# Norm of k and the turns of b, k and v: from the matrix engine to VectorE and 32-partition transfers, in a two-layer hybrid trunk

## The chip, the cores and the metric

The kernel runs on one core of one Trainium2 chip. Time is device microseconds of that core, the median of several runs; the profile is one execution recorded by the hardware profiler. The engines are TensorE (PE, with its weight loads PEld), VectorE (DVE), ScalarE (ACT), GpSimd (POOL) and SyncE (SP, which here only issues transfers).

## The reference, cut to what matters

The input x has 512 rows of 1024 features. Each of two layers runs a norm, one wide projection into all branches, three branches side by side (RWKV-7 time mixing, chunked retention, a spatial gating unit), a gated merge with an output projection, and a gated MLP with a depthwise convolution. The change lies in the RWKV-7 branch (8 heads of 64):

```python
kk = (k * k_k).astype(jnp.float32)
k = k * (1.0 + (a - 1.0) * k_a)
...
kk = kk / jnp.maximum(jnp.sqrt(jnp.sum(kk * kk, axis=-1, keepdims=True)), 1e-12)
y = rwkv7_scan(r, decay, k, v, kk, a)
...
sa = jnp.einsum('bhvk,bhk->bhv', state, -kk_t)
state = (state * w_t[:, :, None, :]
         + sa[..., None] * (kk_t * a_t)[:, :, None, :]
         + v_t[..., None] * k_t[:, :, None, :])
y = jnp.einsum('bhvk,bhk->bhv', state, r_t)
```

So kk is normed by head and time step, and the state is updated 512 times, one step after the other.

## The kernel before, in words

Activations lie with features on the 128 partitions and the 512 time steps along the free axis. Every large product is made three times in a rounded format (`mm3`, L147 to L157: the products of L151, for the parts hi and lo of both sides). A weight unit of 128 x 512 is loaded by SP (`load`, L121, three raw buffers), cut into hi and lo by ACT (L134) and DVE (L135) ahead of its use (`part`), and read by twelve products.

`run` goes through both layers; `mixer` calls `rwkv`. There, a pair of heads (m = 0 to 3) has its columns r, k, v from `cols3(m)`, and `prep(m)` makes the decays, the scaled operands `x` (L494, L495), `bk` (b and k, L498 and L501) and, with TensorE (L507, L510), the products of b and k with the operands by chunks of 64 steps. In `prep`, ACT squares k (L476) into `kkn`; four TensorE products with a matrix of two columns of ones per half sum the squares by head (L479), with the time steps on the partitions; DVE bounds the sums from below into `nw` (L480). After the fourth prep DVE writes the reciprocals into `n2` (L553), by 32-step blocks.

`solve` (L671) inverts the 64 x 64 triangles of all chunks and heads. DVE transposes the blocks (L696) and the norms (L698), scales with them (L699), runs 31 elimination steps (L703, L705), scales again (L706) and transposes back (L708, L710); ACT and POOL copy the diagonal blocks out and in (`diag`, L684, L686). Then TensorE makes two sets of 64 small products (L720, L729), with copies between them.

Then comes the recurrence, chunk by chunk (c = 0 to 7; L581 to L650). It needs b, k and v with time on the partitions. `vpair(c)` turns v of two chunks by four TensorE transposes (L568) into a PSUM bank, from which ACT copies with the halves swapped (L573); per chunk four transposes turn b and k (L590), and ACT copies them out (L601, L603). Small products of `mm` (L563) then do, in each chunk: the products of the state St with `x`; a copy of the result into `xb` by DVE (L599); the products of `xb`, of k and of v; a copy into `U` by ACT (L617); the products of `U`; the state update by DVE (L626, or L628 and L629). The output y is copied by ACT (L633) and normed every two chunks by DVE, with a power on POOL (L648).

Between these small steps `fill` puts units of other work, mostly the gate projections (`gates`), into PE's queue: 35 half-steps during the solve, which may move, and fixed ones of twelve products between the steps of a chunk. The gates go to memory by ACT's queue (L380) and come back in `merge` by POOL's (L934). A planner lays out the instructions of all engines from its own estimated costs; `tc.keep_in_program_order` (`po`) pins an instruction behind the one written just before it on the same engine. The engines then run each queue in that order. Tiles of one tag share a fixed number of buffers: `cs` three, `r` sixteen.

In layer 1's up-projection `turn_x` (L958 to L969) already turns blocks of x: DVE transposes of 32 x 32 blocks (L963), SP transfers to memory (L966) and back in 128-byte pieces (L968).

Of the kernel before, what the change touches and what calls it, by code (L numbers as in the profile page):

```python
# [47 lines left out]
class Emit:  # L48
# [346 lines left out]
    def rwkv(self, l, nst):  # L395
# [15 lines left out]
        n2, nw = self.small((128, 32), "n2"), self.small((128, 4, 4, 2), "nw")  # L411
        Ws = []
        for i in range(2):
            wua, s = self.u(n="wua"), self.u(dt=F32R, n="wus")
# [45 lines left out]
        def prep(m):  # L460


            k, r, v = kc[m], rc[m], Vf[m]
            ms = slice(m * 128, m * 128 + 128)
            pL, pA = self.sm(), self.sm()
            for o, w, (xh, xl) in zip((pL, pA), Ws, Xs):
                T.matmul(o, w[:, ms], xl, start=True, stop=False)  # L467
                T.matmul(o, w[:, ms], xh, start=False, stop=True)  # L468
# [7 lines left out]
            A.activation(kkn, k, AF.Square, scale=self.p("kk", m))  # L476
            pn = self.sm((128, 4, 2))
            for i in range(4):
                T.matmul(pn[:, i, :], kkn[:, i * 128:i * 128 + 128], self.c("bones2"), start=True, stop=True)  # L479
            V.tensor_scalar(nw[:, m], pn, 1e-24, None, op0=MAX)  # L480
            A.activation(ld, pL, AF.Tanh, scale=0.5, bias=haw[:, 4 + m:5 + m])
            A.activation(ld, ld, AF.Identity, scale=-0.5 * EXP_HALF, bias=self.c("ehalf"))
            V.tensor_tensor_scan(ci, self.rst, ld, 0.0, op0=MUL, op1=ADD)
# [12 lines left out]
            V.scalar_tensor_tensor(kkn, tha, 1.0, k, op0=ADD, op1=MUL)  # L496
            A.activation(tha, tha, AF.Identity, scale=hka[:, m:m + 1], bias=oka[:, m:m + 1])
            V.scalar_tensor_tensor(bk[:, :, 0, :], q8(kkn), nkk[:, m:m + 1], q8(Eout), op0=MUL, op1=MUL)  # L498
            kp = k
            V.tensor_tensor(kp, k, tha, op=MUL)  # L500
            V.tensor_tensor(bk[:, :, 1, :], q8(kp), q8(Eout), op=MUL)  # L501
            for g in range(2):
                pB, pK = [self.sm((128, 4, 128)) for _ in range(2)]
                for j in range(4):
                    c = 4 * g + j
                    for h in range(2):
                        i = T.matmul(pK[hv[1 - h], j, :], bk[hv[h], c, 1, :], x[hv[h], c, :], start=True, stop=True)  # L507
# [40 lines left out]
        A.activation(gd, gd, AF.Tanh, scale=0.5)  # L548
        V.tensor_scalar(gd, gd, 0.5, 0.5, op0=MUL, op1=ADD)

        for h in range(2):
            for i in range(2):
                V.reciprocal(n2[hv[h]].rearrange("p (m c i) -> p m c i", m=4, i=2)[:, :, :, i], nw[hv[i], :, :, h])  # L553
        self.pool = None
        self.solve(GB, n2)

        Vt, yT, mh = [None] * 8, [], [(m, h) for m in range(4) for h in range(2)]  # L560

        def mm(o, l, r, start=False):
            po(T.matmul(o, l, r, start=start, stop=True, skip_group_check=True))  # L563

        def vpair(c):
            pv = self.sm((128, 4, 128))
            for m in range(4):
                po(T.transpose(pv[:, m, :], Vf[m][:, c * 64:c * 64 + 128], self.c("ident")))  # L568
            wp = self.rw((128, 2, 4, 64), "cs", 3)
            for i in range(2):  # L570
                Vt[c + i] = wp[:, i]
                for h in range(2):
                    A.copy(wp[hv[1 - h], i], pv[hv[i], :, 64 * h:64 * h + 64])  # L573

        self.fill(1, True)
        vpair(0)
        self.fill(FILL[2], True)
        Q = self.sm((128, 2, 4, 64))
        for m, h in mh:
            mm(Q[hv[h], 1, m, :], Y[m][hv[1 - h], 0, 0:64], Vt[0][hv[1 - h], m, :], m == 0)  # L580
        for c in range(8):  # L581
            if c % 2 == 0:
                y = self.r(n="y")
            if c:
                self.fill(FILL[2], True)
            P1 = self.sm((128, 2, 4, 64))
            if c < 7:
                pb = self.sm((128, 4, 128))
                for m in range(4):
                    po(T.transpose(pb[:, m, :], BK[m][:, c, :, :].rearrange("p a t -> p (a t)"), self.c("ident")))  # L590
                if c % 2 == 0:
                    bts = self.rw((128, 2, 4, 128), "cs", 3)
                bt = bts[:, c % 2]
            if c % 2 == 0 and c < 6:
                vpair(c + 2)
            for m, h in mh if c else ():
                mm(P1[hv[1 - h], 0, m, :], X[m][hv[h], c, 64:128], St[hv[h], m, :], m == 0)
                mm(Q[hv[h], 1, m, :], X[m][hv[h], c, 0:64], St[hv[h], m, :])
            V.tensor_copy(xb, Q[:, 1])  # L599
            if c < 7:  # L600
                A.copy(bt[:, :, 0:64], pb[:, :, 0:64])  # L601
                for h in range(2):
                    A.copy(bt[hv[h], :, 64:128], pb[hv[1 - h], :, 64:128])  # L603
            self.fill(FILL[2], True)
            Q = self.sm((128, 2, 4, 64)) if c < 7 else None
            for i in (0, 4, 5, 6, 7, 1, 2, 3):
                for h in range(2):
                    m, o = i % 4, 1 - h
                    if c < 7 and i < 4:
                        mm(Q[hv[h], 0, m, :], bt[hv[o], m, hv[h]], Vt[c][hv[o], m, :], m == 0)  # L610
                    elif c < 7:
                        mm(Q[hv[h], 1, m, :], Y[m][hv[o], c + 1, 0:64], Vt[c + 1][hv[o], m, :])
                    if i < 4:
                        mm(P1[hv[h], 1, m, :], GB[hv[h], 8 * m + c, 0:64], xb[hv[h], m, :], c == m == 0)
                    else:
                        mm(P1[hv[o], 0, m, :], Y[m][hv[o], c, 64:128], Vt[c][hv[o], m, :])
            A.copy(U, P1[:, 1])  # L617
            self.fill(FILL[2], True)
            for m, h in mh:
                mm(P1[hv[1 - h], 0, m, :], GB[hv[h], 8 * m + c, 64:128], U[hv[h], m, :])  # L620
                if c < 7:
                    mm(Q[hv[h], 0, m, :], bt[hv[h], m, hv[h]], U[hv[h], m, :])
            if c < 7:
                f = F[:, :, c:c + 1].to_broadcast([128, 4, 64])
                if c == 0:
# [42 lines left out]
            self.yrw.append(self.split(t, self.f))  # L668
            yield

    def solve(self, G, n2):  # L671


        V, A, T = self.nc.vector, self.nc.scalar, self.nc.tensor
# [20 lines left out]
        V.memset(flat(TS)[:, 0:1024:33], 1.0)  # L695
        V.transpose(NS, GD.rearrange("p u t -> p t u"))  # L696
        nu = TMP[:, 256:288]
        V.transpose(nu, n2)  # L698
        V.tensor_tensor(NS, NS, nu.unsqueeze(1).to_broadcast([128, 32, 32]), op=MUL)  # L699
        for k in range(31):  # L700
            r, c = 31 - k, k + 1
# [7 lines left out]
        TT = self.rw((128, 32, 32), "cs", 3)  # L709
        V.transpose(TT.rearrange("p u t -> p t u"), TS)  # L710
        diag(TT)
        lo = [slice(64 * h, 64 * h + 32) for h in range(2)]
        hi = [slice(64 * h + 32, 64 * h + 64) for h in range(2)]
        self.fill(FILL[0])
# [6 lines left out]
        for g in range(2):  # L721
            for h in range(2):
                for e in range(2):
                    (V.tensor_copy if h else A.copy)(zs[g][hi[h], e::2], z[g][h][(hi, lo)[e][h], e::2])
        self.fill(FILL[1], True)
        pt = [[self.sm((128, 16, 32)) for _ in range(2)] for _ in range(2)]
        for g, i in [(g, i) for g in range(2) for i in range(16)]:
# [474 lines left out]
```

## Time and profile before

| what | value |
|---|---|
| median of 3 runs | 1737.33 us (1736.18 to 1737.69) |
| the profiled execution | 1736.33 us, span 1734.6 us, granted clock 0.999 |
| DMA busy, mean by 40 slices | 0.1 to 0.5 |
| preparation, layer 0 and 1 | about 46 to 140 us and 905 to 1000 us |
| solve | about 140 to 198 us and 1000 to 1058 us |
| chunks | about 206 to 285 us and 1066 to 1146 us |

The span is the time from the first to the last instruction. A row of the timeline gives start, duration, engine, line, operation and tiles (out<-in). A row of a group gives the busy time in us, the mean duration in ns and the idle time ahead of it with what ended it. A row of one line's instructions gives the shortest, median and longest duration in ns. Records of PE overlap, as products are pipelined.

### The profile page before, as it was taken

The numbers are of one execution on the slowest core, as the hardware profiler recorded it, in microseconds if no ns is written. First come the engines' busy times: TensorE is split into PE (matmuls) and PEld (weight loads), VectorE is DVE, ScalarE is ACT, GpSimd is POOL, SyncE is SP. The second block draws the span as 40 slices with busy tenths as digits, with TensorE's granted clock in tenths as the row PEclk, the third lists the DMA queues.
The fourth block names the chain that finished last, engine by engine and source line by source line (L and its number), as shares of the span: only waits on it lengthen the run. The fifth ranks groups of instructions, "written<-read, shape, count | busy, mean of one in ns | idle before, by whom it ended". The sixth has DMA issues, their size and how long they took to land.

```text
span 1734.6 us, 27538 instructions
## 1 busy us (share of the span) xinstructions
PE 1725.1 (99%) x10544; PEld 1421.0 (82%) x10544; DVE 1121.2 (65%) x1933; ACT 775.8 (45%) x1329; POOL 151.9 (9%) x168
## 2 busy tenths in 40 slices
PE   9999999999999999999999999999999999999998
PEld 7888877888888888888888888778888888888887
DVE  6777645568658777753357785455686698876432
ACT  6554444534345444443255635445343454443322
POOL 1011000002300000000021210000132000000010
PEclk9999999999999999999999999999999999999999
DMA  5234433424543223233332344234154444432431
GB/s 178 86 98 140 134 98 94 134 66 163 162 145 98 97 97 96 69 116 112 116 116 73 98 146 124 92 115 129 59 176 143 152 128 122 121 110 73 152 99 54
DMA packets 124900, 198.64 MB, mean 115 GB/s; under 512 B 29408, under 2 KB 35296, under 8 KB 124768
## 3 DMA queue, kind: packets, MB, share of 16 engines
q1 hardware_dynamic: 110064, 164.15, 30.1%
q10 hardware_dynamic: 10224, 18.05, 3.1%
q0 software_dynamic: 4480, 14.68, 2.6%
q8 instruction: 83, 1.36, 0.3%
q14 instruction: 49, 0.40, 0.1%
HBM read 177.95 MB, written 18.87 MB: 113 GB/s over the span
## 4 chain that ended last, share of the span: by engine, by line
PE 97%; DMA 1%; DVE 1%; ACT 0%; issue 0%; ACTq 0%; DVEq 0%
PE acc L151 86%; PE sm L151 4%; PE sm L563 2%; PE sm L817 1%; PE sm L507 1%; DMA wr<-wall 0%; PE sm L922 0%; PE sm L590 0%; DMA x<-xT 0%; PE sm L479 0%; PE sm L468 0%; PE sm L467 0%; PE sm L845 0%; PE sm L661 0%; PE sm L872 0%
## 5 line engine op out<-in xcount | busy, mean ns | idle before, releaser
L151 PE MATMUL acc<-lo,sh 128*128 128x512 f32 x1108 | 432.6, 391 | 0.0
L151 PE MATMUL acc<-hi,sh 128*128 128x512 f32 x1108 | 431.6, 390 | 0.0
L151 PE MATMUL acc<-hi,sl 128*128 128x512 f32 x1108 | 430.5, 389 | 0.0
L134 ACT CAST sh<-wr 128x512 fp32r<-128x512 f32 (+1 forms) x385 | 235.4, 616 | 390.4 <-PE acc L151 286.8
L135 DVE TENSOR_TENSOR sl<-wr,sh 128x512 fp32r<-128x512 f32 (+1 forms) x385 | 263.4, 688 | 177.9 <-ACT sh L134 108.0
L151 PEld LDWEIGHTS acc<-lo,sh 128*128 128x128 f32 x1108 | 208.0, 188 | 43.9 <-issue 0.7
L151 PEld LDWEIGHTS acc<-hi,sl 128*128 128x128 f32 x1108 | 208.0, 188 | 43.3
L151 PEld LDWEIGHTS acc<-hi,sh 128*128 128x128 f32 x1108 | 208.1, 188 | 42.7 <-issue 0.2
L151 PE MATMUL acc<-lo,wh 128*128 128x512 f32 x588 | 232.9, 396 | 0.8 <-DVE lo L210 0.6
L151 PE MATMUL acc<-hi,wl 128*128 128x512 f32 x588 | 229.7, 391 | 0.0
L151 PE MATMUL acc<-hi,wh 128*128 128x512 f32 x588 | 229.6, 390 | 0.0
L135 DVE TENSOR_TENSOR wl<-wr,wh 128x512 fp32r<-128x512 f32 x195 | 141.8, 728 | 133.8 <-ACT wh L134 132.9
L134 ACT CAST wh<-wr 128x512 fp32r<-128x512 f32 x195 | 120.7, 619 | 218.4 <-PE acc L151 208.0
L151 PEld LDWEIGHTS acc<-lo,wh 128*128 128x128 f32 x588 | 110.5, 188 | 25.8 <-DVE lo L210 1.2
L151 PEld LDWEIGHTS acc<-hi,wl 128*128 128x128 f32 x588 | 110.4, 188 | 23.9 <-issue 0.7
L151 PEld LDWEIGHTS acc<-hi,wh 128*128 128x128 f32 x588 | 110.6, 188 | 22.2 <-issue 0.3
L151 PE MATMUL acc<-ah,sh 128*128 128x512 f32 x352 | 108.4, 389 | 0.0
L989 DVE TENSOR_TENSOR fu<-acc,rsF 128x512 f32<-128x512 f32 x88 | 60.8, 690 | 66.1 <-PE acc L151 66.0
L991 ACT ACTIVATE cv<-fu,pc 128x512 f32<-128x512 f32 x88 | 71.7, 816 | 47.6 <-DVE fu L989 45.1
L992 DVE SCALAR_TENSOR_TENSOR cv<-fu,pc,cv 128x511 f32<-128x511 f32 x88 | 65.7, 748 | 19.9 <-ACT cv L991 19.8
L151 PE MATMUL acc<-wl,hi 128*128 128x512 f32 x192 | 78.3, 408 | 0.0
L151 PEld LDWEIGHTS acc<-ah,sh 128*128 128x128 f32 x352 | 66.1, 188 | 13.6
(297 smaller groups left out, 2338.5 us busy)
## 6 DMA issues: line engine op xcount, KB each, us to landing
wr<-wall SPq DMA_DIRECT2D x488, 256.0 KB, 2.6
gd<-gth ACTq DMA_DIRECT2D x48, 256.0 KB, 2.9
gth<-gd POOLq DMA_DIRECT2D x48, 256.0 KB, 3.5
wr<-wdt SPq DMA_DIRECT2D x44, 256.0 KB, 2.8
wr<-wdn SPq DMA_DIRECT2D x40, 256.0 KB, 2.7
tab<-rot ACTq DMA_DIRECT2D x8, 256.0 KB, 3.5
xi<-xT SPq DMA_DIRECT2D x8, 256.0 KB, 3.3
xd<-xi POOLq DMA_DIRECT2D x8, 256.0 KB, 2.7
```

The source lines that it names most:

```text
L134: self.kept(self.nc.scalar.copy(hi[:, :n], raw[:, :n]))
L135: self.kept(self.nc.vector.tensor_tensor(lo[:, :n], raw[:, :n], hi[:, :n], op=SUB))
L151: i = self.nc.tensor.matmul(*x, **y, **kw)
L507: i = T.matmul(pK[hv[1 - h], j, :], bk[hv[h], c, 1, :], x[hv[h], c, :], start=True, stop=True)
L563: po(T.matmul(o, l, r, start=start, stop=True, skip_group_check=True))
L817: po(T.matmul(X[h][:, i, :], lhsT, rhs, start=new[h], stop=stop, skip_group_check=True))
L989: V.tensor_tensor(u, ps, self.rsF, op=MUL)
L991: A.activation(t, u, AF.Identity, scale=self.p("cw2", j), bias=self.p("cb", j))
L992: V.scalar_tensor_tensor(t[:, 1:], u[:, :511], self.p("cw1", j), t[:, 1:], op0=MUL, op1=ADD)
```

## The change

The sums of squares are made by DVE: `kkn` is transposed in blocks of 32 x 32 and reduced over the 32 features of a block, into `n2`, which now holds half sums. The solve transposes them, brings the two halves of a head together by four small copies on ACT and four additions on DVE, then bounds and inverts them there.

The turns of v (two chunks) and of b and k (two chunks) become `vturn` and `bturn`: DVE transposes blocks of 32 x 32 into a tile z, and transfers inside SBUF, each of 32 partitions, put the blocks into their places in a tile w, those of even destination blocks issued by SP and those of odd ones by GpSimd. A `vturn` is 4 transposes and 8 transfers (pieces of 1 KB); a `bturn` is 8 transposes and 16 transfers (pieces of 128 bytes at the destination). The first ones are written into the solve, the others into chunks 0, 2 and 4 for the two chunks after the next, pinned behind the copy `xb`. The eight transposes on TensorE per two chunks of b and k, the four of v, the PSUM banks that they used and the copies out of them go.

```diff
@@ prep
-            pn = self.sm((128, 4, 2))
-            for i in range(4):
-                T.matmul(pn[:, i, :], kkn[:, i * 128:i * 128 + 128], self.c("bones2"), start=True, stop=True)
-            V.tensor_scalar(nw[:, m], pn, 1e-24, None, op0=MAX)
+            V.transpose(t3[:, 1, :], kkn)
+            V.tensor_reduce(n2[:, :, 8 * m:8 * m + 8], t3[:, 1, :].rearrange("p (c e f) -> p e c f", e=2, f=32), axis=AX.X, op=ADD)
@@ rwkv, after the preps
-        for h in range(2):
...
-                V.reciprocal(n2[hv[h]].rearrange("p (m c i) -> p m c i", m=4, i=2)[:, :, :, i], nw[hv[i], :, :, h])
-        self.solve(GB, n2)
+        def vturn(c):
+            z = self.r((128, 2, 2, 4, 32), n="vz")
+            for m in range(4):
+                (po if c else id)(V.transpose(z[:, :, :, m, :].rearrange("p b i f -> p i b f"), Vf[m][:, c * 64:c * 64 + 128].rearrange("p (i b t) -> p i b t", i=2, b=2)))
+            w = self.r((128, 2, 2, 4, 32), n="vt")
+            for h in range(2):
+                for q in range(2):
+                    for b in range(2):
+                        g, o = 64 * (1 - h) + 32 * b, 64 * h + 32 * q
+                        (nc.gpsimd if b else nc.sync).dma_start(w[g:g + 32, q].rearrange("t i m f -> t (i m f)"), z[o:o + 32, b].rearrange("t i m f -> t (i m f)"))
...
+        def bturn(c):
+            n = min(2, 7 - c)
+            z = self.rw((128, 2, 2, 2, 4, 32), "cs", 3)
+            for m in range(4):
+                for a in range(2):
+                    (po if c else id)(V.transpose(z[:, a, :, :n, m, :].rearrange("p b i f -> p i b f"), BK[m][:, c:c + n, a, :].rearrange("p i (b t) -> p i b t", b=2)))
+            w = self.rw((128, 2, 2, 4, 2, 32), "cs", 3)
...
+                            (nc.gpsimd if b else nc.sync).dma_start(w[g:g + 32, a, :n, :, q, :].rearrange("t i m f -> t (i m) f"),
+                                              z[64 * h + 32 * q:64 * h + 32 * q + 32, a, b, :n].rearrange("p i m f -> p (i m) f"))
...
+        self.solve(GB, n2, lambda: vturn(0), lambda: bturn(0))
@@ the chunks
-            if c < 7:
-                pb = self.sm((128, 4, 128))
-                for m in range(4):
-                    po(T.transpose(pb[:, m, :], BK[m][:, c, :, :].rearrange("p a t -> p (a t)"), self.c("ident")))
...
-            if c % 2 == 0 and c < 6:
-                vpair(c + 2)
...
             V.tensor_copy(xb, Q[:, 1])
-            if c < 7:
-                A.copy(bt[:, :, 0:64], pb[:, :, 0:64])
-                for h in range(2):
-                    A.copy(bt[hv[h], :, 64:128], pb[hv[1 - h], :, 64:128])
+            if c % 2 == 0 and c < 6:
+                vturn(c + 2)
+                bturn(c + 2)
@@ solve
-        V.transpose(nu, n2)
+        nr, ns = self.small((128, 2, 32), "nr"), self.small((128, 32), "ns")
+        V.transpose(nr.rearrange("p e u -> p (e u)"), n2.rearrange("p e u -> p (e u)"))
+        for i, R in enumerate(grp):
+            A.copy(ns[R], nr[grp[i ^ 1], i % 2, :])
+        for i, R in enumerate(grp):
+            V.tensor_tensor(nu[R], nr[R, i % 2, :], ns[R], op=ADD)
+        V.tensor_scalar(nu, nu, 1e-24, None, op0=MAX)
+        V.reciprocal(nu, nu)
...
         diag(TT)
+        turns[0]()
...
+        turns[1]()
         self.fill(FILL[1], True)
```

`turns[0]` is `vturn(0)`, behind the copies of the diagonal blocks; `turns[1]` is `bturn(0)`, behind the copies that follow the first set of solve products. Both are not pinned. The products of the chunk read the new tiles in place of the old ones, with the same count and sizes.

More of the change, by code (lines that the diff above doesn't have):

```diff
@@ L410, in rwkv @@
         V.tensor_scalar(nkk, pcol("kk", 4), -0.5, None, op0=MUL)
-        n2, nw = self.small((128, 32), "n2"), self.small((128, 4, 4, 2), "nw")
+        n2 = self.small((128, 2, 32), "n2")
         Ws = []
@@ L549, in rwkv @@
         V.tensor_scalar(gd, gd, 0.5, 0.5, op0=MUL, op1=ADD)
-        for h in range(2):
-            for i in range(2):
-                V.reciprocal(n2[hv[h]].rearrange("p (m c i) -> p m c i", m=4, i=2)[:, :, :, i], nw[hv[i], :, :, h])
-        self.pool = None
-        self.solve(GB, n2)
-        Vt, yT, mh = [None] * 8, [], [(m, h) for m in range(4) for h in range(2)]
+        self.pool = None
+        Vt, yT, mh = [None] * 8, [], [(m, h) for m in range(4) for h in range(2)]
+        bts = [None] * 7
@@ new lines, in vturn @@
+        def vturn(c):
[8 more added lines that the diff above has]
+                        (nc.gpsimd if b else nc.sync).dma_start(w[g:g + 32, q].rearrange("t i m f -> t (i m f)"), z[o:o + 32, b].rearrange("t i m f -> t (i m f)"))
+            for i in range(2):
+                Vt[c + i] = [w[:, :, i, m, :] for m in range(4)]
@@ new lines, in bturn @@
+        def bturn(c):
[5 more added lines that the diff above has]
+            w = self.rw((128, 2, 2, 4, 2, 32), "cs", 3)
+            for h in range(2):
+                for q in range(2):
+                    for a in range(2):
+                        for b in range(2):
+                            g = 64 * (h ^ a) + 32 * b
+                            (nc.gpsimd if b else nc.sync).dma_start(w[g:g + 32, a, :n, :, q, :].rearrange("t i m f -> t (i m) f"),
+                                              z[64 * h + 32 * q:64 * h + 32 * q + 32, a, b, :n].rearrange("p i m f -> p (i m) f"))
+            for i in range(n):
+                bts[c + i] = [[w[:, a, i, m].rearrange("p q f -> p (q f)") for m in range(4)] for a in range(2)]
@@ L562, in mm @@
+        self.solve(GB, n2, lambda: vturn(0), lambda: bturn(0))
         def mm(o, l, r, start=False):
             po(T.matmul(o, l, r, start=start, stop=True, skip_group_check=True))
-        def vpair(c):
-            pv = self.sm((128, 4, 128))
-            for m in range(4):
[L568 to L571, printed above, removed]
-                for h in range(2):
-                    A.copy(wp[hv[1 - h], i], pv[hv[i], :, 64 * h:64 * h + 64])
@@ L575, in rwkv @@
         self.fill(1, True)
-        vpair(0)
         self.fill(FILL[2], True)
@@ L579, in rwkv @@
         for m, h in mh:
-            mm(Q[hv[h], 1, m, :], Y[m][hv[1 - h], 0, 0:64], Vt[0][hv[1 - h], m, :], m == 0)
+            mm(Q[hv[h], 1, m, :], Y[m][hv[1 - h], 0, 0:64], Vt[0][m][hv[1 - h]], m == 0)
         for c in range(8):
@@ L586, in rwkv @@
             P1 = self.sm((128, 2, 4, 64))
-            if c < 7:
-                pb = self.sm((128, 4, 128))
[L589 to L593, printed above, removed]
-            if c % 2 == 0 and c < 6:
-                vpair(c + 2)
             for m, h in mh if c else ():
@@ L599, in rwkv @@
             V.tensor_copy(xb, Q[:, 1])
-            if c < 7:
-                A.copy(bt[:, :, 0:64], pb[:, :, 0:64])
-                for h in range(2):
-                    A.copy(bt[hv[h], :, 64:128], pb[hv[1 - h], :, 64:128])
+            if c % 2 == 0 and c < 6:
+                vturn(c + 2)
+                bturn(c + 2)
             self.fill(FILL[2], True)
@@ L609, in rwkv @@
                     if c < 7 and i < 4:
-                        mm(Q[hv[h], 0, m, :], bt[hv[o], m, hv[h]], Vt[c][hv[o], m, :], m == 0)
+                        mm(Q[hv[h], 0, m, :], bts[c][1][m][hv[o]], Vt[c][m][hv[o]], m == 0)
                     elif c < 7:
-                        mm(Q[hv[h], 1, m, :], Y[m][hv[o], c + 1, 0:64], Vt[c + 1][hv[o], m, :])
+                        mm(Q[hv[h], 1, m, :], Y[m][hv[o], c + 1, 0:64], Vt[c + 1][m][hv[o]])
                     if i < 4:
@@ L615, in rwkv @@
                     else:
-                        mm(P1[hv[o], 0, m, :], Y[m][hv[o], c, 64:128], Vt[c][hv[o], m, :])
+                        mm(P1[hv[o], 0, m, :], Y[m][hv[o], c, 64:128], Vt[c][m][hv[o]])
             A.copy(U, P1[:, 1])
@@ L621, in rwkv @@
                 if c < 7:
-                    mm(Q[hv[h], 0, m, :], bt[hv[h], m, hv[h]], U[hv[h], m, :])
+                    mm(Q[hv[h], 0, m, :], bts[c][0][m][hv[h]], U[hv[h], m, :])
             if c < 7:
@@ L669, in rwkv_out, with solve @@
             yield
-    def solve(self, G, n2):
+    def solve(self, G, n2, *turns):
         V, A, T = self.nc.vector, self.nc.scalar, self.nc.tensor
```

## The prediction

> **What bounds the kernel now.** I read the page first: how busy each engine is, and the chain that ended last.
>
> ```profile
> span 1734.6 us, 27538 instructions
> ```
> ```profile
> PE 1725.1 (99%) x10544; PEld 1421.0 (82%) x10544; DVE 1121.2 (65%) x1933; ACT 775.8 (45%) x1329; POOL 151.9 (9%) x168
> ```
> ```profile
> PE 97%; DMA 1%; DVE 1%; ACT 0%; issue 0%; ACTq 0%; DVEq 0%
> ```
>
> The matrix engine (PE) has work for 1725.1 of 1734.6 us and makes up 97% of the chain. VectorE (DVE) is at 65%, ScalarE (ACT) at 45%, GpSimd (POOL) at 9%. So a PE instruction that goes shortens the kernel by what it holds up the next one, if nothing else comes late in its place. The whole forecast is the PE time that goes, and then a check of each thing that could be late.
>
> A PE duration is not that price, because the records overlap. The price is read from the starts, in the timeline of PE (columns: start, duration, engine, line, operation). Without a foreign group, products of L151 start 0.23 us apart (209.61 to 209.84 below, and the same inside every unit of twelve).
>
> **What PE loses: the norm.** In each prep, sixteen short products of L479 stand between L468 and the next L151:
>
> ```profile
> 47.93 0.40 PE L468 MATMUL sm<-hi,wus 128*128 128x512 f32 x1
> 48.17 0.95 PE L479 MATMUL sm<-con,cs 128*128 128x2 f32 x8
> 48.98 0.48 PE L151 MATMUL acc<-lo,wh 128*128 128x512 f32 x1
> 49.30 0.40 PE L151 MATMUL acc<-hi,wh 128*128 128x512 f32 x1
> ```
>
> From L468 to the second L151 is 49.30 - 47.93 = 1.37 us; two steps of 0.23 us would have been 0.46. Each group costs 0.91 us, in 4 preps of 2 layers: 8 x 0.91 = 7.3 us.
>
> **What PE loses: the turns.** First v alone (L568), which happens once a layer, ahead of the chunks:
>
> ```profile
> 209.61 0.39 PE L151 MATMUL acc<-hi,wl 128*128 128x512 f32 x1
> 209.84 0.60 PE L568 MATMUL sm<-con,rwc 128*128 128x128 f32 x4
> 210.19 0.48 PE L151 MATMUL acc<-lo,wh 128*128 128x512 f32 x1
> 210.51 0.40 PE L151 MATMUL acc<-hi,wh 128*128 128x512 f32 x1
> ```
>
> 0.90 us less two steps of 0.23: 0.44 us. Then b, k and v together (L590, L568), ahead of the state products of an even chunk, and the same handover from L151 to L563 where no turn stands between:
>
> ```profile
> 236.48 0.39 PE L151 MATMUL acc<-hi,wl 128*128 128x512 f32 x1
> 236.71 0.60 PE L590 MATMUL sm<-con,bk 128*128 128x128 f32 x4
> 237.15 0.60 PE L568 MATMUL sm<-con,rwc 128*128 128x128 f32 x4
> 237.68 0.69 PE L563 MATMUL sm<-S,X 64*64 64x64 f32 x32
> ```
> ```profile
> 228.87 0.39 PE L151 MATMUL acc<-hi,wl 128*128 128x512 f32 x1
> 229.18 0.27 PE L563 MATMUL sm<-cs,cs 64*64 64x64 f32 x1
> ```
>
> 1.20 us less the 0.31 that the handover takes anyway: 0.89 us for the pair, so 0.45 for b and k alone. By the code a layer has the pair in chunks 0, 2 and 4, b and k alone in 1, 3, 5 and 6, and v alone once: 3 x 0.89 + 4 x 0.45 + 0.44 = 4.91 us, 9.8 us for both layers. With the norm, 7.3 + 9.8 = 17.1 us of PE go.
>
> The long record of a transpose invites another price:
>
> ```profile
> L590 PE MATMUL sm<-con,bk 128*128 128x128 f32 x56 | 8.5, 274 | 0.0
> ```
>
> The Trainium skill ("TensorE: Matmul & The Clock Gate", Part 4: PE-mode transpose) gives about 275 ns for a transpose inside a kernel; by that figure the 56 + 32 transposes would be an estimated 24.2 us instead of 9.8, and the gain 31.5. The record here agrees in length (274 ns), but four of them start within 0.44 us, so most of each lies under its neighbours. I keep 9.8.
>
> **What VectorE gains.** The nearest rows are its own transposes and a reduction of the same size:
>
> ```profile
> L963 DVE STREAM_TRANSPOSE xz<-xi 128x128 f32<-128x128 f32 x32 | 7.2, 284 | 0.0
> ```
> ```profile
> L696 DVE STREAM_TRANSPOSE cs<-cs 128x1024 f32<-128x1024 f32 x2 | 4.2, 2094 | 0.0
> ```
> ```profile
> L639 DVE TENSOR_REDUCE s<-y 128x8 f32<-128x512 f32 x8 | 5.5, 682 | 2.5 <-ACT y L633 2.3
> ```
>
> Per prep: a transpose of 512 columns (half of 2.09, 1.05 us) and a reduction (0.68): 1.73 us. Per turn inside the loop: 4 transposes for v and 8 for b and k, 7.2 / 32 = 0.225 us each in a row, 2.7 us. The room for it:
>
> ```profile
> 46.00:140.00 94.00, 94.00 (x650) 77.84 (x649) 69.46 (x118) 55.76 (x92) 18.16 (x19) 1.00 0.30 96
> ```
> ```profile
> 206.00:280.00 74.00, 73.89 (x1068) 58.74 (x1057) 29.62 (x56) 36.96 (x82) 3.28 (x2) 1.00 0.30 96
> ```
>
> (Columns: window, its length, then PE, PEld, DVE, ACT, POOL.) In the preparation DVE goes from 69.5 to about 76 of the 90 us that remain; in the loop from 29.6 to about 38 of 74, while ACT loses its copies out of PSUM. I cost this at nothing because PE has stocked work in both places; if that cover went, the preparation would cost 8 x 1.73 = 13.8 us.
>
> In the loop the twelve transposes stand straight behind the copy xb, and DVE runs in order. Behind them wait the split of the weights (L135), L377, L649 and the state update (L628, L629):
>
> ```profile
> 238.73 0.42 DVE L599 COPY XB<-sm 128x256 f32<-128x256 f32 x1
> ```
> ```profile
> 246.88 0.42 DVE L629 TENSOR_TENSOR S<-S,F 128x256 f32<-128x256 f32 x1
> ```
> ```profile
> 249.30 0.69 PE L563 MATMUL sm<-S,X 64*64 64x64 f32 x32
> ```
>
> xb ends at 239.15, the transposes would end at 241.9, and about 2.7 us of other DVE work follows (four passes, each as long as the 0.68 us reduction above), so DVE is free by 244.6, ahead of the state update, which ends at 247.3. PE asks for the state at 249.30, some 0.5 us earlier without the turn: 1.5 us of cover stay. Nothing is charged.
>
> **The transfers.** A turn's v takes 8 transfers, its b and k 16, of 32 partitions each, half from SP, half from GpSimd. No row shows one inside SBUF. The nearest: SP issues of 64 KB in pieces, a load with the same 128-byte pieces, and GpSimd issues of 128 rows.
>
> ```profile
> L966 SPq DMA_DIRECT2D xr<-xz x32: 325/428/1472, 1390.8 to 1538.4; - x32
> ```
> ```profile
> xt<-xr SPq DMA_DIRECT2D x32, 64.0 KB, 2.6
> ```
> ```profile
> L934 POOL DMA_DIRECT2D gth<-gd x48: 536/542/755, 371.3 to 1324.2; - x48
> ```
> ```profile
> gth<-gd POOLq DMA_DIRECT2D x48, 256.0 KB, 3.5
> ```
>
> SP: 12 issues x 0.43 = 5.2 us a turn. GpSimd: 12 x 0.54 = 6.5 us, or, if the 256 pieces of a b/k transfer count like 256 rows, 8 x 1.08 + 4 x 0.54 = 10.8 us. Landing 2.6 to 3.5 us after issue. The turn in chunk 2 starts at 239.2; v is turned by 240.1 and lands by 240.6 + 2.2 + 3.5 = 246.3 (GpSimd is held by L648 until 240.6), and chunk 3 first reads it at about 253 (its state products at 249.30, 0.6 us of them, a unit of twelve at 0.23, and the handover). b and k land by 255 at the slow end, read in chunk 4, after 262. Both have 6 us or more in hand.
>
> ```profile
> 238.98 1.64 POOL L648 TENSOR_TENSOR rs<-s,con 128x8 f32<-128x8 f32 x1 [44.43 <-DVE s L646]
> ```
> ```profile
> 262.73 0.42 DVE L599 COPY XB<-sm 128x256 f32<-128x256 f32 x1
> ```
>
> Every transfer also stands in SP's queue, which brings the weights:
>
> ```profile
> 238.05 0.33 SPq L121 DMA_DIRECT2D wr<-wall  x1
> ```
> ```profile
> 242.67 0.33 SPq L121 DMA_DIRECT2D wr<-wall  x1
> ```
>
> A load goes out about every 4 us. It may wait 5.2 us of issues and 2.7 us of transposes, 8 us. Three raw buffers are used in turn, so a load is read three units, some 12 us, after its issue; it lands after about 2.6: 9 us in hand, and by the code two split units behind that. Charged: nothing; the bounds are 0 and, if none of the stock were there, 8 us in each of 6 turns.
>
> **The solve.** Its chain gets longer by small steps (four copies on ACT, four additions, a maximum and a reciprocal on DVE), and PE comes to its products earlier by the four norms, 3.65 us.
>
> ```profile
> 191.81 2.74 POOL L686 COPY GB<-cs 32x1024 f32<-32x1024 f32 x2 [49.94 <-DVE cs L710]
> ```
> ```profile
> 198.44 1.34 PE L720 MATMUL sm<-cs,GB 32*32 32x32 f32 x128
> ```
>
> The last operand is there at 194.55, PE arrives at 198.44: 3.9 us in hand. The chain begins with PE's own products of the last prep, so it should move forward with PE. The small steps are bounded by these rows, of larger copies and of the reciprocals that go:
>
> ```profile
> L573 ACT COPY cs<-sm 64x256 f32<-64x256 f32 x32 | 11.7, 366 | 3.1 <-PE sm L568 2.6
> ```
> ```profile
> L553 DVE RECIPROCAL n<-nw x8: 240/248/252, 120.1 to 982.2; 64x16 f32<-64x16 f32 x8
> ```
>
> At most 4 x 0.37 + 6 x 0.25 = 3.0 us. If the chain did not move at all and all of them lay on it, PE would wait 3.65 + 3.0 - 3.9 = 2.75 us a layer, 5.5 us in all; if it moves with PE, nothing. I charge 1.3 us, a quarter, as the chain starts from PE and the squares are complete long before the solve needs them.
>
> **Sum.** 1736.33 (the profiled execution, span 1734.6 and 1.7 around it) - 17.1 + 1.3 = 1720.5 us. The median shown, 1737.33, lies 1.0 above that execution, so the forecast is **1721.5 us**.
>
> **Rivals.** (1) *The preparation turns VectorE-bound*: its bursts are already dense, and the 13.8 us above fall on PE. 1721.5 + 13.8 = 1735, no change that shows. For it: 69.5 of 94 us on average means full stretches. Against: in the last prep the squares were ready 14 us ahead of the scan, so the added steps can fill DVE's waits between. 6 in 100.
>
> ```profile
> 102.75 0.72 ACT L476 ACTIVATE cs<-rwc,pc 128x512 f32<-128x512 f32 x1
> ```
> ```profile
> 117.06 1.66 DVE L483 TENSOR_TENSOR_SCAN cs<-rst,cs 128x512 f32<-128x512 f32 x1
> ```
>
> (2) *The solve ends late*, 4.2 us more than charged, and up to 5 from a planner that lays out all instructions anew: 1726 to 1731. 14 in 100. (3) *GpSimd becomes the bound of the loop, and the kernel slower.* Two chunks last 262.73 - 238.73 = 24.0 us, 22.7 without the turns; GpSimd has 12 issues and 1.64 us of L648 in that time. It is late from (22.7 - 1.64) / 12 = 1.75 us per issue on. With three turns a layer and some 9 us in hand, the gain is gone at about 2.25 us; at 2.5 us the loss is 3 x 8.9 - 9 = 17.8 us a layer, 35.6 in all: 1721.5 + 35.6 = 1757. For it: small pieces have never been issued there. Against: 0.54 us, and four times that is needed. The Trainium skill ("SBUF — State Buffer", SBUF: two separate sides) says that GpSimd cannot write its descriptors while VectorE runs in a mode that takes both ports; no run here shows that yet. By that rule one blocked issue would be an estimated 0.5 plus one DVE pass, about 1.2 us, short of 1.75. 11 in 100. (4) *The transposes are worth their full records*: 31.5 us less, 1707. The starts speak against it. 1 in 100. The forecast, 1717.5 to 1725, has 68.
>
> **Range and chances.** A measurement of this kernel tells about 0.2% (3.5 us) from no change. 1717 to 1731 takes in the forecast and rival 2. Faster by more than 0.2% are the forecast, rivals 2 and 4: 0.83. Within it rival 1: 0.06. Slower rival 3: 0.11.
>
> **What would show it.** Right: L479, L568 and L590 gone, L151 to L563 at 0.31 us, PE without waits, and the span about 16 us shorter, 3.65 us of it before each solve. Rival 1: PE waits for L135, L501 or L521 in the preparation. Rival 2: PE waits ahead of L720's products. Rival 3: PE waits in the chunk for a transfer from GpSimd, with issues above 1.75 us. Wrong altogether: a longer L563 with the new operands, or weight casts waiting for loads in the loop.

## The result and the profile after

| kernel | median (lowest to highest) | profiled execution | ratio to before, 95% interval |
|---|---|---|---|
| before, beside it | 1737.05 us, 4 runs | 1736.33 us, span 1734.6 | |
| changed | 1720.11 us (1719.34 to 1720.37), 4 runs | 1719.34 us, span 1717.6 | 0.9902 (0.9890 to 0.9913) |

The change takes 17 us away, 1%. The forecast was 1721.5 by the median and 1720.5 for the profiled execution. From the first part of the changed kernel's page, the span and the busy times; then the first line of the chain that ended last:

```profile
span 1717.6 us, 27712 instructions
...
PE 1708.1 (99%) x10392; PEld 1403.9 (82%) x10392; DVE 1141.2 (66%) x2041; ACT 750.1 (44%) x1263; POOL 206.6 (12%) x264
...
PE 98%; DMA 1%; DVE 0%; ACT 0%; POOL 0%; issue 0%; ACTq 0%; SPq 0%; DVEq 0%; POOLq 0%
```

PE is busy 17.0 us less and the span is 17.0 us shorter: what left PE left the kernel. All that PE waits for (columns: us in total, times, longest):

```profile
PE acc L274 <- DVE rst L271: 1.5, 1, 1.5
PE acc L151 <- DVE lo L210: 0.9, 2, 0.7
```

Both stood there before (1.5 and 0.6 us). No wait is new, neither for the norm nor for a turn or a transfer. The two places of the norm and of the turn, in PE's timeline:

```profile
48.16 0.39 PE L468 MATMUL sm<-hi,wus 128*128 128x512 f32 x1
48.39 0.39 PE L151 MATMUL acc<-lo,wh 128*128 128x512 f32 x1
...
231.06 0.39 PE L151 MATMUL acc<-hi,wl 128*128 128x512 f32 x1
231.38 0.69 PE L591 MATMUL sm<-S,X 64*64 64x64 f32 x32
```

The step after L468 is 0.23 us as inside a unit, and the state products (old L563, now L591) start 0.32 us behind the last L151 in an even chunk, as the forecast wanted. The work has gone to the other engines, in the preparation and in the recurrence (columns: window, its length, PE, PEld, DVE, ACT, POOL, clock, DMA share, GB/s):

```profile
46.00:140.00 94.00, 94.00 (x634) 77.30 (x633) 73.28 (x129) 56.92 (x96) 21.86 (x21) 1.00 0.33 102
203.00:273.00 70.00, 70.00 (x1026) 54.58 (x1015) 35.69 (x92) 25.99 (x51) 22.96 (x38) 1.00 0.53 135
```

DVE has 73 of 94 us in the preparation. In the recurrence ACT loses its copies (26.0 us busy, 34.8 in the same 70 us of the kernel before) and GpSimd goes from 3.3 to 23 us; the DMA engines are busy 0.53 of the time, in place of 0.30.

The new instructions, on VectorE by line (shortest, median, longest in ns), and one turn in its timeline:

```profile
L477 DVE STREAM_TRANSPOSE cs<-cs x8: 693/702/707, 35.9 to 952.2; 128x512 f32<-128x512 f32 x8
L478 DVE TENSOR_REDUCE n<-cs x8: 660/675/683, 37.1 to 954.0; 128x16 f32<-128x512 f32 x8
```
```profile
129.39 0.89 DVE L557 STREAM_TRANSPOSE vz<-rwc 128x128 f32<-128x128 f32 x4
192.90 1.65 DVE L573 STREAM_TRANSPOSE cs<-bk 128x128 f32<-128x128 f32 x8
```

The issues of the transfers, and their landing:

```profile
L563 SPq DMA_DIRECT2D vt<-vz x32: 507/584/1846, 130.3 to 1110.3; - x32
L563 POOL DMA_DIRECT2D vt<-vz x32: 496/502/727, 130.6 to 1111.1; - x32
L580 POOL DMA_DIRECT2D cs<-cs x64: 548/582/637, 197.0 to 1115.4; - x64
L580 SPq DMA_DIRECT2D cs<-cs x64: 585/612/2010, 197.5 to 1117.9; - x64
```
```profile
cs<-cs POOLq DMA_DIRECT2D x48, 32.0 KB, 3.5
cs<-cs SPq DMA_DIRECT2D x48, 32.0 KB, 3.8
vt<-vz SPq DMA_DIRECT2D x32, 32.0 KB, 2.8
```

### The profile page after: what moved, and what is told of

It is laid out like the page before. It is cut to its first block, busy times and chain, and to the rows that moved or that the text cites. A ratio compares the mean times of both kernels' runs of the same rounds, so it can differ in the third digit from the quotient of the medians.

```text
span 1717.6 us, 27712 instructions
## 1 busy us (share of the span) xinstructions
PE 1708.1 (99%) x10392; PEld 1403.9 (82%) x10392; DVE 1141.2 (66%) x2041; ACT 750.1 (44%) x1263; POOL 206.6 (12%) x264
## 4 chain that ended last, share of the span: by engine, by line
PE 98%; DMA 1%; DVE 0%; ACT 0%; POOL 0%; issue 0%; ACTq 0%; SPq 0%; DVEq 0%; POOLq 0%
PE acc L151 88%; PE sm L151 4%; PE sm L591 2%; PE sm L833 1%; PE sm L505 1%; PE sm L938 0%; DMA x<-xT 0%; DMA ws<-sgw 0%; PE sm L468 0%; PE sm L467 0%; PE sm L861 0%; PE sm L888 0%; PE sm L668 0%; PE sm L812 0%; PE sm L227 0%; PE sm L745 0%
## 5 line engine op out<-in xcount | busy, mean ns | idle before, releaser
L151 PE MATMUL acc<-lo,sh 128*128 128x512 f32 x1108 | 432.7, 391 | 0.0
L151 PE MATMUL acc<-hi,sh 128*128 128x512 f32 x1108 | 431.7, 390 | 0.0
L151 PE MATMUL acc<-hi,sl 128*128 128x512 f32 x1108 | 430.6, 390 | 0.0
L151 PEld LDWEIGHTS acc<-lo,sh 128*128 128x128 f32 x1108 | 208.0, 188 | 43.9 <-issue 0.7
L151 PEld LDWEIGHTS acc<-hi,sl 128*128 128x128 f32 x1108 | 208.0, 188 | 43.6
L151 PEld LDWEIGHTS acc<-hi,sh 128*128 128x128 f32 x1108 | 208.1, 188 | 42.6 <-issue 0.2
L151 PE MATMUL acc<-lo,wh 128*128 128x512 f32 x588 | 232.6, 396 | 0.9 <-DVE lo L210 0.9
L151 PE MATMUL acc<-hi,wl 128*128 128x512 f32 x588 | 229.7, 391 | 0.0
L151 PE MATMUL acc<-hi,wh 128*128 128x512 f32 x588 | 229.1, 390 | 0.0
L135 DVE TENSOR_TENSOR wl<-wr,wh 128x512 fp32r<-128x512 f32 x195 | 137.9, 708 | 112.4 <-ACT wh L134 105.7
L151 PEld LDWEIGHTS acc<-lo,wh 128*128 128x128 f32 x588 | 110.4, 188 | 26.2 <-DVE lo L210 1.9
L151 PEld LDWEIGHTS acc<-hi,wl 128*128 128x128 f32 x588 | 110.4, 188 | 24.1 <-issue 0.7
L151 PEld LDWEIGHTS acc<-hi,wh 128*128 128x128 f32 x588 | 110.5, 188 | 22.0
L151 PE MATMUL acc<-ah,sh 128*128 128x512 f32 x352 | 108.4, 389 | 0.0
L151 PE MATMUL acc<-wl,hi 128*128 128x512 f32 x192 | 78.3, 408 | 0.1
L151 PEld LDWEIGHTS acc<-ah,sh 128*128 128x128 f32 x352 | 66.1, 188 | 13.8
```

The costliest lines, as they stand in the source:

```text
L135: self.kept(self.nc.vector.tensor_tensor(lo[:, :n], raw[:, :n], hi[:, :n], op=SUB))
L151: i = self.nc.tensor.matmul(*x, **y, **kw)
```

## The experiments

All times are medians; the kernel before, run beside each group, had 1737.05 to 1737.35 us.

### The two parts by themselves

The norm alone (the kernel before with the new `prep` and `solve` lines):

> Only the norm moves to VectorE, the turns stay on TensorE. Theory (PE time that goes is the whole gain, and nothing else comes late): 7.3 us under the kernel before, about 1729.8, PE busy down by 7.3. Rival (VectorE becomes the limit of the preparation, or the solve ends late): 1731 to 1737, with PE waiting in 46 to 140 us or ahead of the solve's products.

The turns alone (the changed kernel with the norm on PE as before):

> Only the turns move, the norm stays on TensorE. Theory: 9.8 us under the kernel before, about 1727.2; with the norm-only run the two gains add up to the 17 us of the whole change. Rival (the gain comes from the freed PSUM banks and ACT copies as well): more than 11 us here, and a sum of both gains that differs from 17 by over 2 us.

The norm alone gave 1728.52 us, ratio 0.9950 (0.9937 to 0.9962); the turns alone 1727.28 us, ratio 0.9943 (0.9929 to 0.9956). The busy lines, first of the norm alone, then of the turns alone:

```profile
PE 1717.5 (99%) x10480; PEld 1413.7 (82%) x10480; DVE 1124.8 (65%) x1945; ACT 777.9 (45%) x1337; POOL 153.1 (9%) x168
```
```profile
PE 1715.4 (99%) x10456; PEld 1411.1 (82%) x10456; DVE 1136.8 (66%) x2029; ACT 749.1 (43%) x1255; POOL 206.0 (12%) x264
```

PE's busy time falls by 7.6 us for the norm and by 9.7 us for the turns (forecast 7.3 and 9.8). No new wait of PE in either is longer than 0.5 us. In PE's busy time the two parts simply add: 17.3 us against 17.0 in the whole. The medians fall by 8.8 and 10.0 us, 18.7 together, 1.7 more than the whole; that is within the intervals. The turns alone stay under the 11 us that a gain from the freed PSUM banks and copies would have had to show.

### Who issues the transfers

All 24 of a turn by SP, and all by GpSimd:

```diff
-  (nc.gpsimd if b else nc.sync).dma_start(w[...], z[...])
+  nc.sync.dma_start(w[...], z[...])      # or nc.gpsimd
```

> All 24 transfers of a turn issued by SP, none by GpSimd. SP then has 24 x 0.6 = 14.4 us of issues and some 3 us of weight loads in two chunks of 22.3 us. Theory (the stock of three raw buffers and two split units covers it): the time of the whole change, 1720 within 2 us, with more weight casts waiting for a load. Rival (weights come late behind the transfers): PE waits of 1 to 5 us in each of 6 turns, 1726 to 1750.

> All 24 transfers of a turn issued by GpSimd. At the 0.50 to 0.58 us per issue of the changed kernel that is 13.4 us and 1.7 of the power in 22.3 us. Theory: 1720 within 2 us, GpSimd's busy share about 16%. Rival (GpSimd is held up by VectorE while it issues): issues above 0.9 us, b and k late, PE waits in the chunks, 1725 to 1750.

GpSimd alone: 1720.81 us, ratio 0.9905 (0.9892 to 0.9919), as fast as the half split. SP alone: 1725.18 us, ratio 0.9933 (0.9921 to 0.9946), 5 us worse. PE's first wait with SP alone, and who waited for the transfers of b and k there:

```profile
PE sm L591 <- DVE XB L607: 2.2, 2, 1.3
```
```profile
  DVE wl L135: 6.6, 2
  ACT wh L134: 6.5, 3
```

By the profile the splits of the weights wait 13 us for these transfers (2.7 us in the changed kernel); xb stands behind them in VectorE's order and comes late. So SP's queue was not free: half of the transfers hide, all of them do not. PE's new waits make up about 3 of the 4.4 us that the span grew, and PE's own busy time is 0.9 us longer; where the rest lies stays open.

With all 24 issues on GpSimd, one of b and k still takes 0.58 us, and PE waits for one 0.9 us in one place. From issue to landing they take 2.8 us for v and 3.4 for b and k (medians), against 2.3 and 2.4 with SP alone; why stays open. The Trainium skill ("SBUF — State Buffer", SBUF: two separate sides) would have GpSimd's descriptors wait while VectorE runs an operation that takes both ports; the longest issue of v by GpSimd in the changed kernel took 0.73 us and of b and k 0.64, so no run here shows that wait in the issues.

### The pin behind xb

```diff
-  (po if c else id)(V.transpose(...))
+  V.transpose(...)
```

> The changed kernel, but the twelve VectorE transposes of a turn are not pinned behind the copy xb: the planner may set them where it likes, and sets most of them earlier on VectorE than now (for the second turn, v's four straight ahead of xb, b and k's eight half a chunk ahead). Theory: the place hardly matters, because PE has stocked work; 1720 us, within 2, and no PE wait that is new. Rival: the pin protects xb. In the changed kernel xb ends at 233.52 and PE reads it at 234.95, so 1.4 us are in hand; if v's four (0.88 us) stand ahead nothing is lost, if all twelve do (2.5 us) PE waits 1.1 us in each of 6 turns, 1727, and the waits are of L591 for XB.

1725.30 us, ratio 0.9931 (0.9919 to 0.9943): 5 us of the gain are gone. The rival had the size nearly, and the wrong place: PE waits for the state, not for xb. PE's first wait, and VectorE's timeline in layer 0:

```profile
PE sm L591 <- DVE S L636: 4.5, 2, 2.6
```
```profile
241.52 1.13 DVE L573 STREAM_TRANSPOSE cs<-bk 128x64 f32<-128x64 f32 x8 [5.47 <-DMA cs<-cs]
242.58 0.65 DVE L135 TENSOR_TENSOR wl<-wr,wh 128x512 fp32r<-128x512 f32 x1
243.15 0.41 DVE L635 TENSOR_TENSOR S<-S,sm 128x256 f32<-128x256 f32 x1
243.59 0.42 DVE L636 TENSOR_TENSOR S<-S,F 128x256 f32<-128x256 f32 x1
```

Without the pin the last turn of the layer is set a whole chunk and more ahead of its place, and its first transpose waits 5.5 us for the transfers of the turn before. (That they still read the tile z whose buffer it needs is what the code suggests: `cs` has three buffers. The last of those transfers goes out on SP at 238.96.) The state update stands behind it. So the pin does not act through xb; it keeps the transposes from standing at the head of an in-order queue before they can run.

### b and k turned a chunk later

```diff
-            if c % 2 == 0 and c < 6:
-                vturn(c + 2)
-                bturn(c + 2)
+            if c % 2 == 0 and c < 6:
+                vturn(c + 2)
...
+            if c % 2 and c < 7:
+                bturn(c + 1)
```

> The changed kernel, but b and k are turned a chunk later (behind xb of the odd chunk before their first use) while v stays where it is. The turn's transfers then start at about 245.9, are issued by 250.8 (8 x 0.61 us on SP) and landed by 254.6 (3.8 us), and are read at 257.7: 3 us in hand in place of 11. Theory (a landing of 3.5 to 3.8 us is all there is, and the early turn is no more than a spare): 1720 us, within 2. Rival (transfers land later than the median says, behind loads in SP's queue): PE waits of L591 for cs, some us in each of 6 turns, 1725 to 1735.

1722.59 us, ratio 0.9917 (0.9903 to 0.9930). PE waits for no transfer of b and k, so a landing with 3 us in hand is enough, and the rival is out. The median is 2.5 us above the changed kernel's, a little past what the theory allowed. The profiled execution (1723.79 us, span 1722.1) grew by 4.5 us, and 2.7 of these lie ahead of the first prep, far from the edit: PE reaches the first L467 at 45.2 us in place of 42.5. A wait of L591 for XB is 0.7 us, one for a split of the weights 0.4; where the rest lies stays open.

### Is VectorE full in the preparation?

```diff
+  for _ in range(3):
       V.transpose(t3[:, 1, :], kkn)
       V.tensor_reduce(n2[...], t3[...], axis=AX.X, op=ADD)
```

> The changed kernel with the transpose and the reduction of the norm done three times in each prep (same result): 2 x (0.70 + 0.67) = 2.75 us more VectorE work in each of 8 preps, 22 us in all, so the stretch of 94 us in which VectorE is busy for 73.3 goes to about 84. Theory (VectorE has the room, PE has stocked units): 1720 to 1723 us. Rival (the preparation is close to VectorE-bound, the first rival of the prediction): a large part of the 22 us falls on PE, 1731 to 1742, with PE waits for L135 or for operands that VectorE makes in the preparation.

1722.24 us, ratio 0.9912 (0.9898 to 0.9926): of 21.6 us more VectorE work (1162.8 us busy, from 1141.2) about 2 us at most reach the time. The preparation of layer 0:

```profile
46.00:140.00 94.00, 93.53 (x631) 76.60 (x630) 81.44 (x141) 56.76 (x97) 20.42 (x20) 1.00 0.34 104
```

DVE is busy 81 of 94 us and PE still 93.5. The prediction's first rival (13.8 us on PE) is out by a wide margin.

### Where does GpSimd become the bound?

```diff
-  nc.gpsimd.dma_start(w[g:g + 32, q]..., z[o:o + 32, b]...)
+  for i, m in ((0, 0), (0, 2), (1, 0), (1, 2)):
+      nc.gpsimd.dma_start(w[g:g + 32, q, i, m:m + 2]..., z[o:o + 32, b, i, m:m + 2]...)
... b and k in the same way, by m
```

> The changed kernel with each transfer that GpSimd issues cut in four (by i and m for v, by m for b and k): 48 issues a turn in place of 12, the same bytes; SP's half as it is. At the measured 0.50 us (v) and 0.55 (b, k) that is 16 x 0.50 + 32 x 0.55 = 25.6 us, with the power of L655 27.2, against 22.7 us for two chunks. The prediction's third rival, by its own formula: 25.6 - 21.1 = 4.5 us late a turn, three turns, less 9 us in hand: 4.5 us a layer, 1729. Worked out from the changed kernel's own times: first issue 1.5 us behind xb, 27.2 us of issues, 3 us to land, so 31.7 us behind xb where PE reads at 24.2 behind it: 7.5 us late in the first turn and 4.5 in each of the next two, 16.5 us a layer, 1753, with PE waits of L591 for cs. If GpSimd's issues do not hold anything: 1720.

1761.56 us, ratio 1.0139 (1.0125 to 1.0153): slower than before. PE's waits, and GpSimd's timeline over one turn:

```profile
PE sm L597 <- DMA cs<-cs: 17.7, 8, 6.4
PE sm L597 <- issue: 5.7, 1, 5.7
PE sm L741 <- DVE cs L728: 4.8, 2, 3.8
```
```profile
277.46 7.89 POOL L564 DMA_DIRECT2D vt<-vz  x16
285.35 15.62 POOL L584 DMA_DIRECT2D cs<-cs  x32
```

An issue of a quarter takes 0.49 us, nearly as long as one of the whole (0.50 for v, 0.58 for b and k). The 48 take 23.5 us, with the power 25 us, and two chunks of the changed kernel last only some 22.7. So the mechanism of the prediction's third rival is real, and the changed kernel is spared by its 12 issues of 0.50 to 0.58 us. The rival's own formula (1729) was far too mild, and the finer count (1753) still short. The span grew by 43.1 us: 28 are new waits, and 14.7 are PE's own busy time (1722.8 in place of 1708.1). Of the waits, 4.8 us stand ahead of the solve's products, which no forecast had counted: the 16 issues of the first v come in GpSimd's order (130.14 to 138.19 us in layer 0) ahead of its part in preparing the solve, which begins at 138.25 in place of 134.40. Why PE itself is busy longer is seen in two windows, a stretch with a wait and the next one:

```profile
215.00:225.00 10.00, 6.58 (x81) 5.17 (x80) 4.42 (x16) 1.62 (x3) 9.43 (x19) 0.77 0.51 149
225.00:235.00 10.00, 10.00 (x97) 7.64 (x97) 2.65 (x5) 2.61 (x5) 9.99 (x21) 0.89 0.41 73
```

The granted clock falls to 0.77 in the first, and is still 0.89 in the second, in which PE never rests. A wait of PE costs more than its length.

### More of the same: two further turns

The PE transposes of the retention's q and k (L812) and of y (L668) were moved in the same manner, all issues by GpSimd, 16 per 128 rows:

```diff
+    def turn32(self, x, n):
+        z, w = self.u((128, 4, 4, 32), n="z" + n), self.r((128, 4, 128), n=n)
+        nc.vector.transpose(z.rearrange("p q j f -> p j q f"), x.rearrange("p (j q f) -> p j q f", j=4, q=4))
+        for q in range(4):
+            for b in range(4):
+                nc.gpsimd.dma_start(w[32 * q:32 * q + 32, :, 32 * b:32 * b + 32], z[32 * b:32 * b + 32, q])
```

> The changed kernel, and the rotated q and k of the retention (tile ro) are turned by VectorE and 32-partition transfers too: one transpose of 128x512 per chunk of 128 rows and 16 transfers behind it, all issued by GpSimd, at the end of the recurrence; 16 PE transposes a layer and four copies out of PSUM go. By the starts of the changed kernel the 16 cost 372.37 - 370.17 - 0.46 = 1.74 us a layer, 3.5 us in all. GpSimd is idle from 308 to 344 and has 64 issues of about 0.53 us, 34 us; PE reads the first at 372. Theory (as for the change: PE time that goes is the gain while the transfers have a spare): 1716.6 us, within 2. Rival (the transfers hold the weight loads up, or the issues hold GpSimd's own loads of L950): 1720 or more, with PE waits for L135 or for a load.

> The changed kernel with y turned by VectorE and transfers, ro left on PE: tells the two parts of the run before apart. Theory: 1716.6 us, within 2. Rival: 1720 or more, with PE waits in the loop for S or cs, if the later turn is what costs.

> As the one with ro, and the normalized y of the recurrence is turned the same way at the end of every second chunk: 16 more PE transposes a layer go (4 groups of 0.44 us, 3.5 us in both layers), 16 more GpSimd issues stand in each two chunks (12 x 0.55 + 1.6 + 16 x 0.53 = 16.7 of 22.7 us), and ScalarE's 4 passes of 512 columns become 16 of 128. Theory: 1713 us, within 2. Rival: in VectorE's order the transpose of y and the turn now stand behind the product with rs, which waits for GpSimd's power; the turn and the state update come some 5 us later, and PE waits for S or for cs: 1718 or more.

All three are slower than the kernel before: q and k 1765.88 us, ratio 1.0166 (1.0151 to 1.0181); y 1761.78, ratio 1.0138 (1.0118 to 1.0158); both 1810.67, ratio 1.0430 (1.0414 to 1.0445). The theory, that the PE time that goes is the gain, fell three times, since the spare that it asks for was not there. With q and k, VectorE and PE in layer 0:

```profile
377.45 0.71 DVE L810 STREAM_TRANSPOSE zhT<-ro 128x512 f32<-128x512 f32 x1 [10.31 <-DMA hT<-zhT]
378.09 1.85 DVE L135 TENSOR_TENSOR sl<-wr,sh 128x512 fp32r<-128x512 f32 x3
```
```profile
378.79 0.80 PE L151 MATMUL acc<-hi,sl 128*128 128x512 f32 x1 [9.64 <-DVE sl L135]
379.38 0.63 PE L151 MATMUL acc<-lo,sh 128*128 128x512 f32 x1
379.81 0.63 PE L151 MATMUL acc<-hi,sh 128*128 128x512 f32 x1
...
382.67 0.39 PE L151 MATMUL acc<-hi,sl 128*128 128x512 f32 x1
382.90 0.40 PE L151 MATMUL acc<-lo,sh 128*128 128x512 f32 x1
```

This is the unpinned turn again, larger: a transpose waits 10.3 us for the transfers of the one before, and the weight splits behind it keep PE waiting 9.6 us, and 9.7 in layer 1. These two are about half of what PE waits for anew. The next largest is 12.4 us for L901's activation on ScalarE; its cause stays open:

```profile
PE acc L151 <- DVE sl L135: 19.4, 2, 9.7
PE acc L151 <- ACT sgv L901: 12.4, 2, 6.2
```

With y, the 16 issues go ahead of those of v in GpSimd's queue:

```profile
239.44 8.70 POOL L810 DMA_DIRECT2D yt<-zyt  x16 [2.62 <-DVE gth L377]
...
249.09 1.49 POOL L563 DMA_DIRECT2D vt<-vz  x3 [0.23 <-DMA yt<-zyt]
```
```profile
252.12 1.58 PE L591 MATMUL sm<-vt,Y 64*64 64x64 f32 x30 [3.91 <-DMA vt<-vz]
```

PE waits for v 17.9 us in five places; another 7.5 us are for ScalarE's activation of the retention's v (L772), whose cause stays open too. Neither shows that these turns could not pay in another place or with buffers of their own; that was not tried.

### How much the solve has in hand

```diff
         V.tensor_tensor(TS, TS, nu..., op=MUL)
+        for _ in range(3):
+            V.tensor_scalar(TS, TS, 1.0, None, op0=MUL)
```

> The changed kernel with the chain of the solve made longer: three multiplications of the 128x1024 matrix by 1.0 stand between the last product with the norm (L720) and the transposes (same result). By the nearest rows (a memset of 128x1024 0.91 us, the product itself 1.22) that is 2.7 to 3.7 us a layer. In the kernel before the last operand of the solve was there at 194.55 and PE came at 198.44, 3.9 us in hand; in the changed kernel it is there at 194.98 and PE comes at 194.99. Theory (the chain did not move forward with PE, the whole reserve is used up): PE waits about 2.7 to 3.7 us ahead of the first solve products in each layer, 5.4 to 7.4 us in all, 1725.5 to 1727.5. Rival (as the prediction had it, the chain moves with PE and some reserve is left; the ends of POOL's copies are only modelled): 1720 us, within 2.

1721.01 us, ratio 0.9910 (0.9893 to 0.9926): the chain has 2.1 us more to do in layer 0, PE has no new wait ahead of the solve's products, and the theory falls. The three rows are VectorE's two and PE's one around the first products:

```profile
188.10 2.14 DVE L722 TENSOR_SCALAR cs<-cs 128x1024 f32<-128x1024 f32 x3
...
190.76 2.23 DVE L724 STREAM_TRANSPOSE cs<-cs 128x1024 f32<-128x1024 f32 x1
```
```profile
194.79 1.34 PE L737 MATMUL sm<-cs,GB 32*32 32x32 f32 x128
```

PE starts before the copies of GB (L691 and L693, here at 194.95 and 195.05) do. By the code these products read the tile of the first transpose, not those copies; it is done at 192.99, 1.8 us ahead. In layer 1 it is 5.2 us ahead (1041.47 and 1046.69).

## Why the prediction was right, point by point

**PE's terms: right.** 7.3 and 9.8 us were read from the steps between starts; the two halves alone gave 7.6 and 9.7. (The "sixteen" short products of L479 are eight records in the row shown, from four products in the code; the price came from the starts and does not hang on the count.) The 88 transposes were worth 9.7 / 88 = 0.11 us each. By the price of the Trainium skill ("TensorE: Matmul & The Clock Gate", Part 4: PE-mode transpose), about 275 ns, it would have been an estimated 24.2; no run here bears that out as a price for transposes in a row.

**The charge for the solve: not due, and its ground was wrong.** The prediction took the POOL copy (ending 194.55) for the last operand and saw 3.9 us in hand. The operand is the first transpose. Before, and then in the changed kernel:

```profile
187.51 2.22 DVE L708 STREAM_TRANSPOSE cs<-cs 128x1024 f32<-128x1024 f32 x1
```
```profile
188.29 2.23 DVE L722 STREAM_TRANSPOSE cs<-cs 128x1024 f32<-128x1024 f32 x1
...
194.99 1.34 PE L735 MATMUL sm<-cs,GB 32*32 32x32 f32 x128
```

It ended at 189.73 with PE at 198.44, 8.7 us in hand; now at 190.52 with PE at 194.99, 4.5. And in layer 0 the chain did not "move forward with PE", as the prediction put it: PE comes 3.45 us earlier, the chain ends 0.8 us later. It starts from the last prep's products (L507, now L505), and these run at 131.61 us in place of 130.76, although the norms are gone from PE: other products now stand ahead of them. In layer 1 it did move: the transpose ends at 1037.49 in place of 1049.94, and PE comes at 1046.20 in place of 1058.42, 8.7 us in hand and 8.5 before. The reserve of layer 0 was enough, so the 1.3 us were not due; without them the sum for the profiled execution would have been 1719.2, and 1719.34 was measured.

**VectorE at nothing: right.** Its sizes were too high for the norm (1.73 us a prep; 0.70 + 0.67 = 1.37 measured, because the row of 128x1024 that the transpose was taken from runs at 2.09 us and not at twice 0.70) and fair for a turn (2.7; 0.89 + 1.65 = 2.54). The tripled norm shows the cover.

**The transfers at nothing: right in sum, loose in size.** SP's issues take 0.58 us for v and 0.61 for b and k (medians) and not 0.43, GpSimd's 0.50 and 0.58 as the lower figure had it, and landing takes 2.8 to 3.8 us (2.6 to 3.5). The reserve on SP was smaller than it looked: ACT's casts into wh wait 15.0 us for weight loads in place of 7.7. Of these, 3.0 us in each layer fall into the chunks, where there were none before. The prediction had named such waits as a sign of being wrong altogether; they came, and did not reach PE. With twice the issues on SP the loss is 5 us.

```profile
ACT wh L134 <- DMA wr<-wall: 15.0, 10, 3.0
```

**The pin** was not priced. The prediction costed only the place that it gives the transposes, as a risk (1.5 us of cover left before the state update). The pin is worth 5 us, by keeping the transposes off the queue's head until their buffer is free.

**The rivals.** The first is out (the tripled norm), the second did not occur, the fourth is out by the turns alone. The third is the one that can happen; its threshold (12 issues of 1.75 us, 21 us a turn) was right in kind, as 48 issues of 0.49 us pass it. Its price was too low: it gave 9 us for both layers, where the new waits were 28, and it left out the fall of the granted clock, with which PE's own busy time grew by 14.7.

## What to carry to other kernels

On a kernel that PE bounds, price a removed PE instruction by the steps between starts, and then look for the queue in which its replacement can block. A replacement that runs on an in-order engine must stand where its buffers and operands are already free, and small transfers must be counted as issues (0.5 to 0.6 us each here) against the period in which they are due. An edit that paid once does not pay again by itself: the reserve is spent per queue and per stage.

## What the hardware showed that was not expected

After a wait of 9.6 us PE's products start 0.43 us apart in place of 0.23, for 3.6 us (378.79 to 382.37 in the kernel with q and k turned), and then run as before. The granted clock is 0.50 from 370 to 380 us and 0.87 from 380 to 390. The Trainium skill ("TensorE: Matmul & The Clock Gate", Part 1: The HAM clock gate) says that a rested array runs at half rate until it has been busy for about 3.4 us; the trace agrees, with steps of 1.9 times the length for 3.6 us.

An issue has a price of its own: 0.49 us for 8 KB and 0.50 to 0.58 us for 32 KB on GpSimd, 0.58 to 0.61 on SP. And the transfers take the DMA engines' time out of proportion to their bytes: in the recurrence the rate goes from 96 to 135 GB/s, the busy share from 0.30 to 0.53.
